# Holding the first store of an add-and-GELU kernel back by half a multiply

## The chip, the cores and the metric

The kernel runs on one core of one Trainium2 chip. The metric is the device time of one execution in microseconds (us). A time quoted for a kernel is the median of its executions; a ratio is the mean time of one kernel's runs over the mean of the other's runs of the same rounds, so it is not quite the ratio of the medians. Each experiment was timed together with the kernel before, in alternating rounds on one chip; such a session is called a call below, and times are compared within a call where that is possible. A profile is one execution, taken by the hardware profiler; its span is about 2.2 us shorter than the time of the same execution (119.75 us against 121.92).

## The reference

```python
batch, dim = 1024, 4096          # x, y: float32
z = x + y
out = 0.5 * z * (1 + np.tanh(np.sqrt(2 / np.pi) * (z + 0.044715 * z ** 3)))
```

## The kernel before

x, y and the result lie in HBM, the main memory of the chip; the work is done in SBUF, the memory of the core, on 128 partitions of 32,768 columns each, with `w`, a buffer in PSUM, between the steps. x is loaded into `z`, y into a pair of buffers, and the sum and everything after it is done in 16 chunks of 2048 columns: an add (POOL, chunk 0 on DVE), a square (ACT), a fused add-and-multiply (DVE), a sigmoid (ACT) and the last multiply (DVE) that leaves the result in `z` (0.5 z (1 + tanh u) is z times the sigmoid of 2u). All loads and stores are issued by the sync engine (SP), in this order:

```python
    loads = [2048, 6144, 8192, 8192, 8192]      # columns; x and y alternate
    FIRST = 8
    stores = [16384, 8192, 4096, 4096]
    # [...]
    def store(i):
        a, b = sr[i]
        ins = nc.sync.dma_start(out=ov[:, a:b], in_=zt[:, a:b])
        if i == 0:
            tc.add_manual_dep(
                ins.ins,
                muls[FIRST].name,
                mybir.DependencyInfo(mybir.DependencyClass.Sync, mybir.DependencyReason.DATA),
                reason="the stores join the queue when the last load is nearly done",
            )
    # [...]
    def mul(c):
        a, b = cr[c]
        muls[c] = nc.vector.tensor_mul(out=zt[:, a:b], in0=wt[c], in1=zt[:, a:b]).ins
    # [...]
    for c in range(0, C, 2):
        dve += [(stt, c), (stt, c + 1), (mul, c), (mul, c + 1)]
```

The first store covers chunks 0 to 7, which are ready after multiply 7. It waits, on purpose, for multiply 8 as well. A store is issued as one instruction (0.35 us on SP for the first); one row moved is a packet in the trace (the first store has 128, of 64 KB each, 8 per DMA engine), and the order for one row is called a descriptor below.

Of the kernel before, what the change touches and what calls it, by code (L numbers as in the profile page):

```python
# [61 lines left out]
def kernel(  # L62
# [14 lines left out]
    nc = tc.nc  # L77
# [14 lines left out]
    CH = 2048  # L92
    PS = 2
    loads = [2048, 6144, 8192, 8192, 8192]
    FIRST = 8
    stores = [16384, 8192, 4096, 4096]

    def ranges(sizes):
# [8 lines left out]
    def over(rs, lo, hi):  # L107
        return [i for i, (a, b) in enumerate(rs) if a < hi and b > lo]
# [7 lines left out]
    zt = pool_sb.tile([P, TOT], fp32, tag="z", name="z")  # L116
    yt, wt, muls = {}, {}, {}
# [12 lines left out]
# [8 lines that stand above are left out]
# [24 lines left out]

    def mul(c):
        a, b = cr[c]
        muls[c] = nc.vector.tensor_mul(out=zt[:, a:b], in0=wt[c], in1=zt[:, a:b]).ins  # L165


    sp = []
# [6 lines left out]
    for c in range(0, C, 2):  # L175
        dve += [(stt, c), (stt, c + 1), (mul, c), (mul, c + 1)]
        acts += [(sig, c), (sig, c + 1)]
        if c + 2 < C:
            acts += [(sq, c + 2), (sq, c + 3)]
# [7 lines left out]
        ],  # L187
        add: lambda c: [(f, i) for i in over(lr, *cr[c]) for f in (load_x, load_y)],
        sq: lambda c: [(add, c)] + ([(mul, c - PS)] if c >= PS else []),
        stt: lambda c: [(sq, c)],  # L190
        sig: lambda c: [(stt, c)],
        mul: lambda c: [(sig, c)],
        store: lambda i: [(mul, c) for c in over(cr, *sr[i])] + [(mul, FIRST)],
    }
    queues = [sp, pool, acts, dve]
# [52 lines left out]
```

## Time and profile before

| | kernel before |
|---|---|
| time, 6 runs (3 of them known at the prediction) | 121.80 us (121.49 to 122.04) |
| span of the profile | 119.8 us |
| busiest compute engine | DVE, 62% |
| 16 DMA engines | 98.6% of the span, 50.33 MB |
| first store issued | 76.44 us |
| first add on the last load | 80.91 us |

The row that matters is the DMA row: the engines are hardly without work between the first load and the last store (98.6% of the span), so with the same bytes to move only two things can shorten the time, a DMA engine that gets through its packets faster, or a shorter head or tail. The prediction shows the lines.

One view used throughout is the trace's record of single DMA packets, which has a start, a duration and a size for every packet. A record doesn't name its engine; the packets are strung into 16 chains by each one starting within some nanoseconds of the end of the one before it. A row of a load of 8192 columns is one packet of 32 KB (1.213 to 1.22 us undisturbed); each DMA engine moves 8 rows of such a load, so the last load is 8 packets per engine. "The last load packet but one" is the seventh of them.

### The profile page before, as it was taken

Reading aid. Unit: us, or ns where it says so; the run is one execution under the profiler, and the core shown is the slowest. Engines: PE = TensorE matmul, PEld = TensorE weight load, DVE = VectorE, ACT = ScalarE, POOL = GpSimd, SP = SyncE. Lnnn points to the kernel's source line nnn. Section 1 sums busy time; section 2 is a strip of 40 time slices with the busy share of each in tenths; the row PEclk is TensorE's granted clock in tenths of the full one; section 3 lists DMA queues with packets and bytes.
Section 4 is the critical chain, followed back from the end, with each engine's and each line's share of the span. In section 5 each row is a group of like instructions: output and inputs, shape, how many; then the busy total and the mean of one; then the engine's idle time right before and its main releaser. Section 6 shows DMA issues by size and latency. Waiting matters only on the chain.

```text
span 119.8 us, 174 instructions
## 1 busy us (share of the span) xinstructions
DVE 73.7 (62%) x34; ACT 61.0 (51%) x34; POOL 67.5 (56%) x19
## 2 busy tenths in 40 slices
DVE  0053600004999970749999949999993999990000
ACT  4006000009779706197797668888819879800000
POOL 0000000699980199999869999939999990000000
DMA  6999999989898999989898989998899889999996
GB/s 186 421 487 402 476 435 394 514 361 493 383 493 383 438 438 394 482 361 514 350 525 350 525 350 493 383 525 350 350 613 438 350 350 427 449 405 405 427 432 257
DMA packets 2016, 50.33 MB, mean 420 GB/s; under 512 B 224, under 2 KB 224, under 8 KB 224
## 3 DMA queue, kind: packets, MB, share of 16 engines
q1 hardware_dynamic: 2016, 50.33, 98.6%
HBM read 33.55 MB, written 16.78 MB: 420 GB/s over the span
## 4 chain that ended last, share of the span: by engine, by line
DMA 50%; POOL 26%; POOLq 4%; DVE 4%; DVEq 2%; ACT 2%; SPq 1%; issue 0%
DMA y<-in_y_dram 50%; POOL z L145 26%; POOLq L215 4%; DVE w L156 2%; DVEq L215 2%; DVE z L165 2%; ACT w L150 2%; SPq L121 1%; SPq L128 1%; POOLq L145 0%
## 5 line engine op out<-in xcount | busy, mean ns | idle before, releaser
L145 POOL TENSOR_TENSOR z<-z,y 128x2048 f32<-128x2048 f32 x15 | 67.3, 4519 | 31.1 <-DMA y<-in_y_dram 31.1
L156 DVE SCALAR_TENSOR_TENSOR w<-w,z 128x2048 f32<-128x2048 f32 x16 | 36.7, 2296 | 26.4 <-ACT w L150 26.1
L150 ACT ACTIVATE w<-z 128x2048 f32<-128x2048 f32 x16 | 30.1, 1882 | 38.3 <-POOL z L145 29.3
L165 DVE TENSOR_TENSOR z<-w,z 128x2048 f32<-128x2048 f32 x16 | 35.8, 2281 | 0.0
L161 ACT ACTIVATE w<-w 128x2048 f32<-128x2048 f32 x16 | 29.7, 1855 | 4.4 <-DVE w L156 4.4
L145 DVE TENSOR_TENSOR z<-z,y 128x2048 f32<-128x2048 f32 x1 | 2.3, 2293 | 6.1 <-DMA y<-in_y_dram 6.1
L200 ACT ACT_TABLE_LOAD x1 | 1.3, 1283 | 1.3 <-PEq L232 1.3
L199 DVE MEMSET one<- 128x1 f32 x1 | 0.1, 59 | 1.3 <-PEq L232 1.3
L232 POOL MEMSET const-float32-0.0<- 128x1 f32 x1 | 0.1, 98 | 0.2 <-issue 0.2
L200 ACT ACTIVATE one<-one 128x1 f32<-128x1 f32 x1 | 0.2, 203 | 0.0
L232 POOL MEMSET const-bfloat16-1.0<- 128x1 bf16 x1 | 0.1, 101 | 0.0
L232 POOL MEMSET const-uint8-127<- 128x1 uint8 x1 | 0.1, 101 | 0.0
L232 POOL MEMSET const-float32-1.0<- 128x1 f32 x1 | 0.1, 98 | 0.0
## 6 DMA issues: line engine op xcount, KB each, us to landing
z<-in_x_dram SPq DMA_DIRECT2D x3, 4096.0 KB, 34.6
y<-in_y_dram SPq DMA_DIRECT2D x3, 4096.0 KB, 25.3
out_dram<-z SPq DMA_DIRECT2D x1, 4096.0 KB, 22.2
out_dram<-z SPq DMA_DIRECT2D x2, 2048.0 KB, 14.1
z<-in_x_dram SPq DMA_DIRECT2D x1, 3072.0 KB, 13.4
y<-in_y_dram SPq DMA_DIRECT2D x1, 3072.0 KB, 20.3
z<-in_x_dram SPq DMA_DIRECT2D x1, 1024.0 KB, 4.9
y<-in_y_dram SPq DMA_DIRECT2D x1, 1024.0 KB, 6.9
```

The costliest lines, as they stand in the source:

```text
L121: nc.sync.dma_start(out=zt[:, a:b], in_=xv[:, a:b])
L128: nc.sync.dma_start(out=yt[s][:, o : o + b - a], in_=yv[:, a:b])
L145: eng.tensor_add(out=zt[:, a:b], in0=zt[:, a:b], in1=yt[s][:, o : o + b - a])
L150: nc.scalar.activation(out=wt[c], in_=zt[:, a:b], func=act.Square, scale=root)
L156: nc.vector.scalar_tensor_tensor(out=wt[c], in0=wt[c], scalar=c1, in1=zt[:, a:b], op0=alu.add, op1=alu.mult)
L161: nc.scalar.activation(out=wt[c], in_=wt[c], func=act.Sigmoid)
L165: muls[c] = nc.vector.tensor_mul(out=zt[:, a:b], in0=wt[c], in1=zt[:, a:b]).ins
L199: nc.vector.memset(one, 0.0)
L200: nc.scalar.activation(out=one, in_=one, func=act.Sigmoid)
L215: tc.compile()
L232: nc = _bacc.Bacc("TRN2", target_bir_lowering=False, num_devices=1)
```

## The change

The intent: let the first store join the queue a little later, but not as late as a whole further multiply would make it. Chunk 9's multiply is split into two halves, and the store waits for the first.

```diff
-    FIRST = 8
+    FIRST = 9
@@
     def mul(c):
         a, b = cr[c]
-        muls[c] = nc.vector.tensor_mul(out=zt[:, a:b], in0=wt[c], in1=zt[:, a:b]).ins
+        parts = 2 if c == FIRST else 1
+        n = (b - a) // parts
+        for o in range(0, b - a, n):
+            ins = nc.vector.tensor_mul(
+                out=zt[:, a + o : a + o + n],
+                in0=wt[c][:, o : o + n],
+                in1=zt[:, a + o : a + o + n],
+            )
+            muls.setdefault(c, ins.ins)
```

## The prediction

> **What bounds the kernel now.** I read the page first, then the chain of waits that ended last, the waits of the DMA queue, a table by stages (windows), the timeline around the first store, and last the trace's record of single DMA packets.
>
> ```profile
> span 119.8 us, 174 instructions
> DVE 73.7 (62%) x34; ACT 61.0 (51%) x34; POOL 67.5 (56%) x19
> DMA  6999999989898999989898989998899889999996
> q1 hardware_dynamic: 2016, 50.33, 98.6%
> HBM read 33.55 MB, written 16.78 MB: 420 GB/s over the span
> ```
>
> No compute engine is above 62%, while the 16 DMA engines are busy for 98.6% of the span. The kernel moves 50.33 MB and takes as long as moving them takes. The row of tenths shows no hole: loads up to about 80 us, then stores to the end.
>
> The chain of waits tells another story, and I don't follow it:
>
> ```profile
> 80.91 4.51 POOL z L145
> 85.42 4.49 POOLq L215
> 89.91 8.96 POOL z L145 x2
> 98.87 0.02 issue
> 98.89 1.89 ACT w L150
> 100.78 0.02 issue
> 100.81 2.30 DVE w L156
> 103.11 2.19 DVE z L165
> 105.29 2.20 DVEq L215
> ```
>
> It ends with the last multiply at 107.5 us, because it is a chain of instructions and the last instruction only issues a store. The span goes on for 12 us after that. The timeline has the four stores issued at 76.44, 87.60, 98.57 and 107.52 us; the packet records have the store before each of the last three still moving until about 99.8, 109.5 and 114.3 us. So every later store joins the queue 7 to 12 us before its turn. The arithmetic could be several us late after 80 us and nothing would end later. What sets the end is: when the loads are through, plus 16.78 MB of stores without a hole.
>
> ```profile
> SPq L132 <- DVE z L165: 46.4, 4, 16.5
> 69.63:72.05 2.42, 0.81 (x2) 2.04 (x2) 2.42 (x2) 1.00 0.98 420
> 72.05:74.46 2.41, 2.41 (x2) 1.81 (x2) 2.41 (x2) 1.00 1.01 435
> 74.46:76.88 2.42, 2.42 (x2) 2.03 (x2) 2.42 (x1) 1.00 1.01 433
> 76.88:79.58 2.70, 2.70 (x2) 2.11 (x2) 2.06 (x1) 1.00 1.09 388
> 79.58:82.00 2.42, 2.35 (x2) 2.42 (x2) 1.09 (x1) 1.00 1.00 433
> ```
>
> The first line says that the store queue waits for the multiplies (46.4 us in four waits); of these the first is the one that the change touches. The windows are cut so that each holds two 32 KB load packets of each engine (the last: one 64 KB store packet); the last column is GB/s. The rate is 433 to 435 everywhere except in one place: 388 between 76.88 and 79.58, the 2.7 us right after the first store was issued. In the packet records a load packet of 32 KB takes 1.213 us on nearly every engine at nearly every time, but the ones that started between 76.9 and 79.1 took up to 1.94 us. The excess over 1.213 us, summed and divided by 16, is 0.53 us per engine: the only loss in the record between 3 and 118 us. The packets themselves follow each other without a gap, and the store packets start at 79.60 to 80.46 us, each right behind its engine's last load.
>
> ```profile
> 74.13 4.48 DVE L165 TENSOR_TENSOR z<-w,z 128x2048 f32<-128x2048 f32 x2
> 76.44 0.35 SPq L132 DMA_DIRECT2D out_dram<-z  x1
> 78.53 4.66 DVE L156 SCALAR_TENSOR_TENSOR w<-w,z 128x2048 f32<-128x2048 f32 x2
> 80.91 4.51 POOL L145 TENSOR_TENSOR z<-z,y 128x2048 f32<-128x2048 f32 x1 [1.96 <-DMA y<-in_y_dram]
> ```
>
> These are multiplies 8 and 9, the first store 0.03 us after multiply 8 (74.13 + 2.28 = 76.41), and the first add on the last load, at 80.9.
>
> [...] on every engine the first store packet comes after the last load packet, although it was issued 3.2 us earlier. So holding the store back cannot reorder anything; it can only change what the engines do while it is in the queue. [...] the first load is issued at 0.00 and its first packets start between 1.03 and 1.5 us. [...]
>
> **The change part by part.** *The store's wait.* Before: multiply 8's end, 76.41. After: the end of the first half of multiply 9. Multiplies 8 and 9 are two instructions in 4.48 us, so the second starts 4.48 - 2.28 = 2.20 us after the first, at 76.33. The half has 1024 elements; [...] It ends at 77.54, and the store is issued at about 77.57: 1.13 us later. The order of the store queue does not change. Had the whole multiply been taken, the store would come at 78.65.
>
> *The split.* [...] The slot that multiply 9 frees is taken by a square that starts at 78.97 on POOL's data anyway, 0.36 us after the multiply's end at 78.61; so this is hidden. The comparison of the two programs shows one or two more semaphores to wait on (a square also on ACT's own, the second store also on POOL's); both events lie earlier than the wait that binds. I count zero.
>
> *Does the store come too late?* Its packets can start 1.03 to 1.5 us after the issue: 78.6 to 79.1. Without any slowing the last load packets would end 2 x 1.213 us after 76.89 to 77.35, so at 79.3 to 79.8. The margin is 0.2 to 1.2 us: thin, but no hole is expected.
>
> *What can be won.* The 0.53 us by which the loads slow when the first store arrives. The slow stretch begins about 0.9 us after the issue (packets that end by 77.3 are still at 1.22 us) and the first of the two packets has most of it: 0.46 us of 0.53. After the change the arrival is at about 78.5, when each engine has only 0.8 to 1.3 us of load left.
>
> **The rivals.** *A: the slowing is paid once, by whatever load packet is there when the store's descriptors arrive.* For it: nearly all of it is in one packet per engine. Then it moves from the last but one packet to the last, and the time stays: 121.9. *B: the slowing grows with the load work that the store meets.* For it: the later stores (87.6, 98.6, 107.5 us), which meet stores, and the later loads (35.6, 36.0, 59.5), which meet loads, slow nothing, so it is a matter of a store meeting loads; and somebody had a reason to hold the store back at all. Then of 0.53 us some 0.2 to 0.5 go: 121.4 to 121.7. *C: the store comes too late for some engines.* For it: the margin of 0.2 us at the tight end, and an execution in which the loads run a little ahead. Each engine left dry adds its hole to its own end, and the slowest engine counts: 122.0 to 122.4. Against it: the engine that ends last (80.46) has the largest margin. *D: the multiply chain becomes the bound.* Against it: 6 us of slack after 80 us; I give it nothing.
>
> **Range and chances.** A 0.40, B 0.45 with about 121.55 in the middle, C 0.15 with about 122.2: the mean is 0.40 x 121.92 + 0.45 x 121.55 + 0.15 x 122.2 = 121.8, the median a little lower. I say 121.75 us. The three runs of before span 0.27 us, so the range is A to B's best, widened by that spread: 121.35 to 122.15. Two per cent are 2.4 us; the whole disputed cost is 0.53 us, and a hole of 2.4 us would need the store to be 3 us late. Within 2%: 0.98.
>
> **What would show it right or wrong.** The first store at 77.5 to 77.6; a half multiply of about 1.21 us; the later stores within 0.2 us of where they were; DMA busy still at 98 to 99%. Under A the window of the last two load packets still shows about 388 GB/s and the first add on the last load starts at 80.9; under B the rate there is nearer 433 and the add starts at 80.4 to 80.7; under C the packet records show a gap between the last load packet and the first store packet on some engines. It would be wrong if the rate after 80 us changed, or if a later store found the queue empty.

The half multiply was put at 1.21 us, by a rate per element that no trace had shown, and the sum came to 76.33 + 1.21 = 77.54 us for its end and 77.57 for the issue of the store. The second half was put at about 0.07 us more of DVE: that is what it calls hidden, and it counts zero. The trace of the changed kernel has 1.212 us for the half, and 4.54 us for multiply 8 and the two halves where multiplies 8 and 9 took 4.48. That there is no faster rate to win than the 433 to 437 GB/s of the full stretches was the author's estimate and is not shown. The order of loads and stores is read from one trace there; in that of the changed kernel, too, each engine's first store packet comes after its last load packet, by 0.001 to 0.004 us, with the store issued 2.1 us before the first of them.

## The result, and the profile after

The changed kernel took 121.19 us (121.06 to 121.54, 6 runs), the kernel before 121.80 us (6 runs). The ratio is 0.9958, with a 95% interval of 0.9937 to 0.9979: a small gain that is clear of zero. The prediction had said 121.75 us; the median lies 0.16 us below the lower end of its range, 121.35.

The page of the changed kernel; as before, DMA is the row that is full:

```profile
span 119.4 us, 175 instructions
DVE 73.7 (62%) x35; ACT 61.0 (51%) x34; POOL 67.5 (57%) x19
q1 hardware_dynamic: 2016, 50.33, 98.6%
```

The timeline around the first store, and the group of the half multiplies from the table by shape (start us, duration us, or: busy us and mean ns):

```profile
74.03 4.54 DVE L168 TENSOR_TENSOR z<-w,z 128x2048 f32<-128x2048 f32 x3
77.46 0.35 SPq L132 DMA_DIRECT2D out_dram<-z  x1
80.50 4.51 POOL L145 TENSOR_TENSOR z<-z,y 128x2048 f32<-128x2048 f32 x1 [1.68 <-DMA y<-in_y_dram]
...
L168 DVE TENSOR_TENSOR z<-w,z 128x1024 f32<-128x1024 f32 x2 | 2.3, 1212 | 0.0
```

The store is issued at 77.46 in place of 76.44, the half takes 1.212 us, and POOL gets the last load at 80.50 in place of 80.91. The windows of two load packets per engine, cut at the starts of that execution's packets (last column GB/s):

```profile
74.75:77.17 2.42, 2.42 (x2) 2.03 (x2) 2.42 (x1) 1.00 1.02 433
77.17:79.59 2.42, 2.42 (x3) 1.85 (x2) 1.65 (x1) 1.00 1.01 433
79.59:82.01 2.42, 2.42 (x2) 2.35 (x2) 1.51 (x1) 1.00 1.00 433
```

The window of the last two load packets, which had 388 GB/s and 2.70 us before, has 433 GB/s and 2.42 us. The slow stretch is gone. In the packet records the last load packet but one took 1.68 us in the mean before and 1.22 now.

Those two traces alone don't prove that this is the gain. They are single executions and differ elsewhere too: the first loads, in packets of 8 KB, were through 0.21 us earlier in the changed kernel's trace, and small delays on load packets between 35 and 77 us cost it about 0.4 us per engine that the other trace did not have.

### The profile page after: what moved, and what is told of

It reads as the page before. It is cut to its first block, busy times and chain, and to the rows that moved or that the text cites. A ratio compares the mean times of both kernels' runs of the same rounds, so it can differ in the third digit from the quotient of the medians.

```text
span 119.4 us, 175 instructions
## 1 busy us (share of the span) xinstructions
DVE 73.7 (62%) x35; ACT 61.0 (51%) x34; POOL 67.5 (57%) x19
## 4 chain that ended last, share of the span: by engine, by line
DMA 50%; POOL 26%; POOLq 4%; DVE 4%; DVEq 2%; ACT 2%; SPq 1%; issue 0%
DMA y<-in_y_dram 50%; POOL z L145 26%; POOLq L223 4%; DVE w L156 2%; DVEq L223 2%; DVE z L168 2%; ACT w L150 2%; SPq L121 1%; SPq L128 0%; POOLq L145 0%
## 5 line engine op out<-in xcount | busy, mean ns | idle before, releaser
L168 DVE TENSOR_TENSOR z<-w,z 128x2048 f32<-128x2048 f32 (+1 forms) x17 | 35.9, 2154 | 0.0
L145 DVE TENSOR_TENSOR z<-z,y 128x2048 f32<-128x2048 f32 x1 | 2.3, 2291 | 5.8 <-DMA y<-in_y_dram 5.8
```

The source lines that it names most:

```text
L145: eng.tensor_add(out=zt[:, a:b], in0=zt[:, a:b], in1=yt[s][:, o : o + b - a])
L168: ins = nc.vector.tensor_mul(out=zt[:, a + o : a + o + n], in0=wt[c][:, o : o + n], in1=zt[:, a + o : a + o + n],)
```

## The experiments

Two theories at the start. *Arrival*: the slow stretch is paid when the store's descriptors come into a queue of loads. *Growing*: loads run slower for as long as a store waits behind them. A third came out of the experiments 1 to 4, which were run together. Each row of the table is one kernel; the packet columns are from its one trace, the time columns from its runs. "Loads end" is the mean over the 16 engines of the end of the last load packet.

| kernel | store issued | last load packet but one, mean (max) | last, mean | loads end | time of that execution | median | ratio to before, same rounds |
|---|---|---|---|---|---|---|---|
| before | 76.44 | 1.68 (1.94) | 1.28 | 80.08 | 121.92 | 121.80 | |
| changed | 77.46 | 1.22 (1.29) | 1.21 | 79.81 | 121.53 | 121.19 | 0.9958 |
| changed, again | 77.55 | 1.22 (1.22) | 1.22 | 79.51 | 121.32 | 121.22 | 0.9971 |
| split only | 76.33 | 1.22 (1.22) | 1.27 | 79.56 | 121.43 | 121.48 | 0.9998 |
| store after multiply 7 | 68.02 | 2.05 (2.24) | 1.23 | 80.32 | 122.14 | 121.90 | 1.0028 |
| half of multiply 8 | 75.33 | 1.96 (2.36) | 1.26 | 80.30 | 122.16 | 122.02 | 1.0036 |
| quarter of multiply 9 | 76.92 | 1.24 (1.33) | 1.21 | 79.50 | 121.30 | 121.36 | 0.9985 |
| three quarters of 9 | 77.97 | 1.22 (1.22) | 1.22 | 79.53 | 121.33 | 121.31 | 0.9985 |
| whole multiply 9 | 78.54 | 1.22 (1.22) | 1.22 | 79.49 | 121.35 | 121.43 | 0.9989 |
| before, second trace | 76.35 | 1.72 (1.88) | 1.22 | 80.04 | 121.78 | | |
| before, third trace | 76.38 | 1.22 (1.22) | 1.24 | 79.61 | 121.36 | | |

One reading needs no theory: time minus loads' end is 41.7 to 41.9 us in every row. The end of the loads sets the time, and what follows is stores without a hole (nearly so in the kernel that waits for the whole of multiply 9, experiment 3).

### 1. The split alone

```diff
-    FIRST = 9
+    FIRST = 8
-        parts = 2 if c == FIRST else 1
+        parts = 2 if c == 9 else 1
```

> Multiply 9 in two halves, but the first store still waits for multiply 8. Theory (the time of the store's arrival is what counts): the same time as before, 121.8 us within 0.15, the store issued at about 76.4, and the slow stretch of load packets right after it is there again, about 0.5 us per engine. Rival (the split itself or the changed semaphores help, or the stretch was an accident of one execution): near the changed kernel's 121.2 us.

Measured: 121.48 us against 121.61 of the kernel before, ratio 0.9998 (0.9976 to 1.0019). So the split by itself gains nothing. But half of the expectation failed: the trace of this kernel has almost no slow stretch, although its store was issued at 76.33:

```profile
76.88:79.34 2.46, 2.46 (x3) 1.88 (x2) 1.95 (x1) 1.00 1.01 426
```

Either the split has to do with it, or a store at that time is sometimes harmless; experiment 9 settles this.

### 2. The store as early as it can go

```diff
-    FIRST = 8
+    FIRST = 7
```

> The kernel before with no extra wait: the first store is issued when multiply 7 is done, at about 68.1 us, some 8 us earlier than in the kernel before. Theory 1 (one slow stretch when a store's descriptors arrive in a queue of loads, whenever that is): 121.8 us as before, with about 0.5 us per engine lost at 69 to 71 us and nothing at 77 to 79. Theory 2 (loads run slower all the time that a store waits behind them): 0.53 us were lost in some 2.5 us, so about 2 us in 10.5 us; about 123.5 us, with a lower rate from 69 us to the end of the loads.

Measured: 121.90 us (121.82 to 122.14), ratio 1.0028 (1.0010 to 1.0047). Both theories fall: *arrival* names about the right time and the wrong place, *growing* a time that is 1.6 us too long. The timeline and the windows of this kernel:

```profile
68.02 0.35 SPq L132 DMA_DIRECT2D out_dram<-z  x1
81.10 4.52 POOL L145 TENSOR_TENSOR z<-z,y 128x2048 f32<-128x2048 f32 x1 [2.29 <-DMA y<-in_y_dram]
...
76.78:80.09 3.31, 3.31 (x2) 2.73 (x2) 2.03 (x1) 1.00 0.99 317
80.09:82.50 2.41, 2.34 (x2) 2.41 (x2) 1.40 (x1) 1.00 1.01 435
```

The store is issued 8.4 us earlier than in the kernel before, and the slow stretch is not at 69 us, where the *arrival* theory puts it; it is at 76.78 to 80.09, in the same two packets of the queue as before. The packets of the 8 us in between are at 1.22 to 1.23 us in the mean, so it does not grow either. The packet records put all of it in one place: the last load packet but one takes 2.05 us on the mean engine (1.75 to 2.24), 0.84 us too long, and the last one is normal again.

The theory that this suggests, *place in the queue*: an engine that begins its last load packet but one loses about 0.84 us in the mean if, by then, the store stands behind the loads. When it came there makes no difference, and if it comes later nothing is lost.

### 3. Waiting for the whole of multiply 9

```diff
-    FIRST = 8
+    FIRST = 9
```
(and no split)

> The whole multiply 9 is waited for, no split: the store is issued at about 78.65 us and its packets can start at 79.7 at the earliest, while the engines end their loads at 79.6 to 80.1. If a late store leaves a hole: gaps of 0.1 to 0.5 us between the last load and the first store packet, and 121.3 to 121.7 us, slower than the changed kernel by 0.1 to 0.5. If the store's first packets need less lead than that: as the changed kernel, 121.2 us, no gap.

Measured: 121.43 us (121.35 to 121.59), ratio 0.9989 (0.9971 to 1.0007), so not clear of the kernel before. The loads are clean, and the store comes too late for some engines:

```profile
78.54 0.35 SPq L132 DMA_DIRECT2D out_dram<-z  x1
...
76.82:79.26 2.44, 2.44 (x2) 1.86 (x2) 2.01 (x1) 1.00 1.00 430
```

The packet records show four engines through with their loads at 79.26 to 79.35 that all start on the store at 79.39: 0.85 us after the issue, with gaps of 0.04 to 0.13 us; a fifth waits 0.09 us. After that the store packets took 2.427 us in the mean, not 2.418. Its executions lie 0.2 us above those of the changed kernel of the same call without overlap (121.17 to 121.32); its one trace accounts for about 0.05 of that, the rest I can't place.

### 4. The changed kernel again

> The changed kernel again, on the chip of this call: about 0.6 us under the kernel before, 121.2 us, no slow stretch at 77 to 80 us, no gap ahead of the store packets. If its first trace was a lucky one: a slow stretch here, and a time nearer 121.8.

Measured: 121.22 us (121.17 to 121.32), ratio 0.9971 (0.9954 to 0.9989). The gain holds in a second call, 0.39 us of medians there and not the expected 0.6. Its trace is clean: no load packet of the last two above 1.221 us.

### 5. Half of multiply 8: a little earlier than the kernel before

The split of the changed kernel moved to chunk 8, with `FIRST = 8` there.

> Multiply 8 is done in two halves and the first store waits for the first of them: issued at about 75.3 us, in the queue of the engines by about 76.2 (0.85 us from issue to first packet, as seen where a store came to engines that had nothing else to do). The engines begin their last load packet but one at 76.9 to 77.3 us. Theory (an engine loses about 0.84 us in its last load packet but one if a store stands behind it in the queue by then, and it makes no difference for how long): as with the store after multiply 7, about 0.7 us above the changed kernel in every execution, last load packet but one at about 2.05 us on all engines. Rival (the loss grows with the time that the store waits): between the kernel before and the one with the store after multiply 7, at most 0.5 us above the changed kernel, several packets a little longer.

```profile
75.33 0.35 SPq L132 DMA_DIRECT2D out_dram<-z  x1
...
74.49:76.91 2.42, 2.42 (x3) 1.95 (x2) 2.42 (x1) 1.00 1.01 433
76.91:80.00 3.09, 3.09 (x2) 2.60 (x2) 1.98 (x1) 1.00 1.04 339
```

Measured: 122.02 us (121.75 to 122.22), ratio 1.0036. Issued 1.1 us before the kernel before, it has nearly the whole loss (1.96 us per last load packet but one; 1.50 to 2.36 on single engines, so not the same on all of them), close to the 2.05 us of the store issued 8.4 us before the kernel before. This is the *place in the queue* theory's prediction, and the *growing* one's failure.

### 6. A quarter, and three quarters, of multiply 9

```diff
-        parts = 2 if c == FIRST else 1
-        n = (b - a) // parts
-        for o in range(0, b - a, n):
+        cuts = [0, 512, b - a] if c == FIRST else [0, b - a]     # 1536 in the other kernel
+        for o, e in zip(cuts, cuts[1:]):
+            n = e - o
```

> Multiply 9 in two parts of 512 and 1536 elements, the store waits for the first: issued at about 77.0 us, at the engines at 77.9, just after they have begun their last load packet but one. Theory: as the changed kernel within 0.1 us, at most a few last load packets at 1.45 us. Rival (the loss grows with the time of waiting, or is spread about the arrival): halfway between the kernel before and the changed one, about 0.2 us above the changed one.

> Multiply 9 in parts of 1536 and 512 elements, the store waits for the first: issued at about 78.1, at the engines at about 78.9, after they have begun their last load packet (78.1 to 78.6) and before the first of them is through (79.3). Theory (any arrival between 77.4 and 79.3 is as good as another): as the changed kernel, 0.3 to 0.5 us below the kernel before, no slow packet and no gap. If the store needs more lead than 0.85 us: a gap, and the time of the kernel that waits for the whole of multiply 9.

Measured: 121.36 us (121.25 to 121.52) and 121.31 us (121.30 to 121.36), each with ratio 0.9985 (0.9969 to 1.0000 and 0.9972 to 0.9999). Both traces are clean:

```profile
76.86:79.30 2.44, 2.44 (x3) 1.86 (x2) 1.95 (x1) 1.00 1.01 430
```

that of the quarter, and for three quarters

```profile
76.77:79.21 2.44, 2.44 (x3) 1.85 (x2) 2.03 (x1) 1.00 1.00 430
```

So the traces show a plateau: a store issued anywhere from about 77 to 78 us finds almost nothing to lose, and the half of the change sits in its middle. The times are a weaker witness. Neither kernel beats the changed one, and the gains are smaller than its 0.39 us: 0.26 us for the quarter, where the kernel before had the same median as in the repeat (121.62 and 121.61), and 0.19 for three quarters (121.50), where 0.3 to 0.5 was expected. They are from other calls than the changed kernel's, and what makes this difference was not tested.

### 7. Is it the volume of the store?

```diff
-    stores = [16384, 8192, 4096, 4096]
+    stores = [2048, 14336, 8192, 4096, 4096]
-        if i == 0:
+        if i < 2:
-                muls[FIRST].name,
+                muls[7 if i == 0 else FIRST].name,
```

> A small first store (2048 columns, rows of 8 KB, 1 MB) is issued when multiply 7 is done, at about 68 us; the rest of the first store (14336 columns) waits for the first half of multiply 9 as in the changed kernel. If the loss comes with any store that stands behind the loads: about 0.7 us above the changed kernel, last load packet but one at about 2.05 us. If it is the volume of the store's row [...]: 0.84 x 8/64 = 0.1 us, so about as the changed kernel.

```profile
76.83:79.78 2.95, 2.95 (x3) 2.37 (x2) 2.11 (x1) 1.00 1.01 355
```

Measured: 121.91 us (121.75 to 122.20), ratio 1.0030. A store of 1 MB in rows of 8 KB, an eighth of the big store's rows, costs 0.4 us in the last load packet but one and 0.13 in the last, together about 0.53 us, not 0.1. So the loss is not in proportion to the store's rows; a small one behind the loads has some two thirds of it.

### 8. Smaller packets at the end of the loads

```diff
-    loads = [2048, 6144, 8192, 8192, 8192]
-    FIRST = 8
+    loads = [2048, 6144, 8192, 8192, 6144, 2048]
+    FIRST = 7
```

> The store after multiply 7 (always there in time), and the last pair of loads cut into 6144 and 2048 columns, so that the last load packets of an engine have 8 KB in place of 32. If the loss sits a fixed number of packets ahead of the store: it is in the last packet but one, of 8 KB, which then takes 0.3 + 0.84 us. If it sits a fixed number of bytes ahead: it is some four to eight packets earlier. In both cases 121.9 us within 0.2; if the loss shrinks with the packet, 121.3 to 121.5.

Measured: 121.89 us (121.77 to 122.00), ratio 1.0026. The last load now ends in packets of 8 KB (0.31 us). From the last backwards they took about 310, 320, 340, 400, 410, 370, 330 ns in the mean, up to 645 ns: the slow ones are mainly the fourth to the sixth from the end. So it is neither "the last packet but one" as such, nor the same stretch of bytes as with 32 KB packets. These packets lost only about 0.3 us, but the loads ended at 79.97 us all the same. I have no control for what the two added DMAs cost, so this run says where the slow packets are and nothing on the size of the loss. Its trace also has loads in rows of 8 KB behind loads in rows of 24 KB: no packet of 24 KB there is above 0.925 us (0.916 in the mean), so smaller rows behind larger ones do not cause the loss by themselves.

### 9. Is the kernel before always slow there?

The kernel before, unchanged, traced twice more.

> The kernel before, unchanged, for a second trace. In its first trace the last load packets but one took 1.68 us in the mean (0.46 us too long); with the store after multiply 8 and multiply 9 merely split they took 1.22. Theory (its store is at the engines at about 77.3, just as they begin that packet, so it is chance from execution to execution): a mean anywhere between 1.22 and 2.05 us, and the time goes with it, 121.3 to 122.1. If the two halves of multiply 9 were what made the split kernel's trace clean: again about 1.68 us here.

> A third trace of the kernel before; the same expectation: under the theory of chance it differs from the other two, with the loads ending up to 0.8 us earlier or later; under the rival again about 1.68 us for the last load packet but one.

The second trace has 1.72 us, the third 1.22. The timeline and the last two load packets of the second:

```profile
76.35 0.35 SPq L132 DMA_DIRECT2D out_dram<-z  x1
...
76.92:79.81 2.89, 2.89 (x2) 2.32 (x2) 1.91 (x1) 1.00 1.02 363
```

and of the third:

```profile
76.38 0.35 SPq L132 DMA_DIRECT2D out_dram<-z  x1
80.35 4.52 POOL L145 TENSOR_TENSOR z<-z,y 128x2048 f32<-128x2048 f32 x1 [1.49 <-DMA y<-in_y_dram]
...
76.97:79.41 2.44, 2.44 (x2) 1.87 (x2) 1.90 (x1) 1.00 1.01 430
```

The same program, a store issued within 0.1 us of the others, and no slow stretch. Its loads end 0.47 us earlier than in the first trace, and the execution took 121.36 us against 121.92. So the split is not needed for a clean trace, which answers experiment 1, and the kernel before loses about 0.5 us at this place in some executions and next to nothing in others.

I read this as a race. The store is issued at 76.35 to 76.44; with the 0.85 us of experiment 3 it is, as an estimate, at the engines at 77.2 to 77.3, and the engines begin their last load packet but one at 76.9 to 77.35. But that is not shown, and its simple form does not fit: in the second trace the engines begin that packet 0.58 to 0.94 us after the issue and all 16 are slow (1.42 to 1.88 us), in the third 0.60 to 0.94 us after it and none is. If each engine raced against a store that comes 0.85 us after its issue, both traces would have some slow and some clean engines. So something decides that is much the same for all engines and that the issue and start times don't show. A way from issue to engines that takes longer in one execution than in another would do it, as a guess; no run measures it behind loads.

The times alone would not have told it either. Over the three calls of timed runs and the last single one the kernel before ran 121.30 to 122.09 us, and the changed kernel's six runs of the repeat span only 0.15 us; but in the first comparison they span 0.48 us (121.06 to 121.54), almost as much as the 0.55 us of the kernel before.

### 10. Reading SBUF or writing HBM?

```diff
+    spare = pool_sb.tile([P, CH], fp32, tag="spare", name="spare")
+    def copy(i):                      # issued between the last load and the first store
+        ins = nc.sync.dma_start(out=spare, in_=zt[:, :CH])
+        tc.add_manual_dep(ins.ins, muls[7].name, ...)
```

> In place of the small early store, a copy of the same size and rows (2048 columns, 8 KB) from SBUF to an unused SBUF tile stands behind the loads from about 68 us; the real first store waits for the first half of multiply 9. The copy adds 1 MB and so about 2.4 us to the whole. [...] the last load packet but one at about 1.6 us as with the small early store. If it has to do with writing to HBM: 1.22 us there, loads through at 79.3 to 79.8.

The first case: what slows the last loads is that the data are taken from SBUF.

```profile
68.05 0.52 SPq L144 DMA_DIRECT2D spare<-z  x1
...
76.89:79.73 2.84, 2.84 (x3) 2.27 (x2) 1.95 (x1) 1.00 1.06 369
```

Measured: one run, 124.57 us beside 121.82 of the kernel before; about 2.5 us of the difference are the copy's own packets (8 per engine of 0.309 us). The last load packets but one took 1.57 us (up to 1.99) and the last 1.43: 0.56 us lost, the loads end at 80.11. That is what the small early store did, and the copy writes nothing to HBM (the first real store was issued at 77.48, as in the changed kernel, where it costs nothing). In this one trace a transfer that takes its data from SBUF is enough, if it stands behind a queue of loads. Loads behind loads do nothing of the kind: at the border of the last two loads, at 69 to 70 us, the packets are at 1.22 us in the mean, and at 1.24 in the first trace of the changed kernel, where those at 67 to 69 us have 1.23 as well.

## Why the prediction was wrong

**What bounds the kernel** was right. In all kernels of the table the time is the end of the loads plus 41.7 to 41.9 us, and the slack of the arithmetic after 80 us was never used up. (One line was misread: the rate is not "433 to 435 everywhere except in one place", for the first window shown has 420. Its packets are at 1.22 us like the others; 420 GB/s is 31 packets of 32 KB in the window in place of 32, an effect of where it is cut.)

**The change's own parts** were right: 77.57 predicted and 77.46 measured for the issue (the pair of multiplies had started 0.10 us earlier), 1.21 and 1.212 us for the half. The split gains nothing by itself (experiment 1, 0.9998). The later stores came 0.4 us earlier in two cases, not within 0.2, because the last load was there earlier; nothing depends on it.

**The step that failed is what becomes of the 0.53 us when the store comes later.** The term was named and put in the right place, but both accounts of it were wrong. Rival A, "the slowing is paid once, by whatever load packet is there when the store's descriptors arrive", had 0.40 of the chances and kept the whole term, so the time near 121.9. Experiment 2 shows that arrival costs nothing: a store that came 8 us earlier left the packets of that time at 1.22 us and slowed those at the end of the queue. Rival B, "the slowing grows with the load work that the store meets", leaned to the gain, but by the wrong mechanism: half of multiply 8 and multiply 7 differ by 7 us of waiting and hardly at all in loss (0.78 and 0.84 us). From it came the step "of 0.53 us some 0.2 to 0.5 go". In the changed kernel's trace all of it went: the last two load packets are 0.01 us over their normal time. The store was not there yet when the engines came to the place where it costs. All the signs named for B came true (433 GB/s in the window, the add at 80.50) and none of those for A and C; that the prediction leaned the right way by B was luck, since B's reason is refuted.

**The size of the term was taken from one trace.** In three traces of the kernel before it was 0.52, 0.50 and 0.02 us, and 0.78 to 0.84 where the store was there early enough. With one trace its size could not be known; the second of the unchanged kernel happened to agree with it, and only the third showed that it varies.

**The sum of the range was not what its words say.** "A to B's best, widened by that spread" is 121.4 - 0.27 to 121.92 + 0.27, so 121.13 to 122.19; 121.35 to 122.15 was written. The wider range would have held the result, but not for a better reason.

**Not all of the fall is accounted for.** The whole term taken off the 121.92 of the trace of before leaves 121.39, not 121.19. In the repeat the medians differ by 0.39 us, which the term can cover; in the first comparison by 0.61. The traces also differ by up to 0.25 us in the first loads, and the changed kernel's first trace has 0.4 us of small delays that the others don't have; its runs at 121.1 have no trace. So how much of the first comparison's gain is the term and how much such scatter stays open.

**Rival C** (too late) was right to be small: the trace with the whole multiply 9 gives 0.85 us from issue to first packet, where the prediction had 1.03 to 1.5 from the program's first load. By that, an estimate from the issues at 77.46 and 77.55, the store was at the engines at about 78.3 to 78.4 in the two traces of the changed kernel, and they needed it at 79.3 at the earliest.

**What stays open** is what the DMA engine does in that packet. The loss lies ahead of the SBUF-sourced packets and not in them: they take 2.418 us in the mean both in the first trace of the kernel before, where 0.52 us were lost, and in that of the changed kernel, where 0.01 were, so they don't give the loss back. Why the load packet takes so much longer, no run here shows.

## What to carry to other kernels

Where one DMA queue goes from loads to stores and the DMA engines are the bound, look at the packet durations just ahead of the change: here a store that stood behind the loads too early cost up to 0.84 us in the last load packets, and one issued too late left holes of 0.04 to 0.13 us. Between the two lay at least one microsecond (issues at 76.92 to 77.97 us had neither). When an effect sits at one place in a single trace, trace the unchanged kernel again, more than once, before giving it a size (here one trace had 0.52 us and another 0.02), and move the suspected cause far away (here 8 us earlier) to see whether the effect goes with it.

## What the runs measured along the way

- From HBM loads to SBUF-sourced transfers in one queue: a store in rows of 64 KB behind loads in rows of 32 KB cost 0.78 to 0.84 us per engine in the last two load packets where it was issued at 68.02 or 75.33 us, nearly all of it in the last but one; a store or an SBUF copy in rows of 8 KB, issued at 68 us, cost 0.53 to 0.56 us. Loads behind loads showed nothing of the kind (1.22 to 1.24 us per packet at 69 to 70 us).
- From issue to first packet: 0.85 us from the start of the issuing instruction, 0.50 from its end, on engines that had just run out of loads (experiment 3), and 1.03 us from the start for the first load of the program (first trace of the kernel before).
- A fp32 tensor_tensor on DVE: the one add with both inputs in SBUF took 2293 ns for 2048 elements, the multiplies with one input in PSUM 2281 (2291 and 2280 in the changed kernel), and 1212 for 1024. What makes the 11 to 12 ns between add and multiply was not tested.
